# A decoder layer's two norms: token blocks multiplied before their norm, and norm weights applied per channel after the transposes

## Chip, cores and metric

The kernel runs on one core of a Trainium2 chip. The metric is device time in microseconds (us) for one execution. TensorE (PE) multiplies matrices and transposes, VectorE (DVE) and ScalarE (ACT) work elementwise, GpSimd (POOL) does small odd jobs, SyncE (SP) issues most of the transfers. SBUF is the on-chip memory, PSUM the eight banks that PE writes; a bank here holds 128 partitions x 512 float32.

## What is computed

One layer on 512 tokens of 1024 channels: an RMS norm, a combined input projection, a convolution branch and a gated linear attention branch, a gated merge with an output projection and a residual, a second RMS norm, a gated feed-forward of width 2816 with a short convolution, a residual, a last norm. The change touches the two norms and what reads them:

```python
def _rmsnorm(x, g):
    y = x * lax.rsqrt(jnp.mean(x * x, axis=-1, keepdims=True) + EPS)
    return y * g

u = _rmsnorm(h, norm1_g)
proj = u @ w_in                 # [conv GLU | q | k | v | r | decay | gates]
...
h = h + merged @ w_o
u2 = _rmsnorm(h, norm2_g)
z = _causal_dwconv(u2 @ w_ffn_up, ffn_dw_w, ffn_dw_b)
```

## The kernel before

Every float32 product is made of three fast ones: each operand is split into a high part (`hi`, a cast by ACT) and a remainder (`lo`, a subtraction by DVE), and `mm3` (L294) multiplies lo*hi, hi*lo and hi*hi into one bank. The tokens are four blocks of 128. Weights come as tiles of 128x1024 (512 KB): SP loads them into `raw` (four buffers), ACT casts `whi` (L253), DVE subtracts `wlo` (L256), and the load that takes the freed buffer is issued behind that. `order` fixes the sequence of weights, `split_weight` and `prefetch` keep the splits ahead of the products.

The start is ordered by hand for PE, ACT, DVE and SP (`manual_schedule`, L393). SP loads the first norm's weights as one row, x of block 0, two tiles of w_v, x of block 1, further weights. PE spreads the row over 128 partitions with two matmuls (L404) and does three warm-up matmuls (L408). `norm1(t)` squares and sums x (ACT, L413), adds epsilon (DVE), raises to -0.5 (POOL, L346) and multiplies x by the root and the weights (DVE, L419). `to_channels` (L369) transposes a block (PE, L375, two banks of four 128x128 pieces), casts (ACT, L379) and subtracts (DVE, L380) into `u1`, which holds hi and lo of all tokens by channel. `values(0, next_tokens)` then makes the first 512 columns of v: block by block, each over all eight channel groups with the four w_v tiles, 96 products; behind the fourth channel group of each block the next one is transposed and the one after it normed. Then come the GLU weights with all 512 tokens as the moving operand.

The output projection runs through `seven` (L823), a scheme of seven products on quarters: steps a11, a12, s1, n2, s4, n3, a22. Each step takes two token blocks (i = 0, 1); s4, n3 and a22 end with twelve products for each block, in banks x, y and z. A finished bank is added to or taken from `hres`, the residual stream (DVE, L870), and n3 and a22 write the banks x one after the other. `hres` is loaded again from x by SP (L881), behind the second norm's weights, which SP loads spread over 128 partitions (`load_gain`, 512 KB). `o_complete` squares and sums (ACT, L886) and takes the root (POOL); `norm2` multiplies by root and weights (DVE, L898); `o_at` places block 0's and 1's scaling behind n3's first block and their transposes behind a22's two blocks. The last w_o pieces are summed in memory by POOL's accumulating transfers (`kept`, L224).

The feed-forward's first group multiplies four tiles of w_up (L1044 to L1051) by the first 256 tokens and then by the last 256, since blocks 2 and 3 are normed last; these are transposed behind the third and fourth tile's first half.

## Time and profile before

| | before |
|---|---|
| median of 3 runs | 846.5 us (846.46 to 846.63) |
| profiled execution, span | 845.6 us |
| PE busy | 830.7 us (98%) |
| DVE busy | 646.0 us (76%) |
| ACT busy | 383.2 us (45%) |
| POOL busy | 42.6 us (5%) |
| first product of w_v starts at | 10.69 us |
| first product of w_glu starts at | 36.43 us |

The span reaches from the first to the last instruction of one profiled execution; the runs' times are taken without a profile. In a row by time stand start, duration, engine, line, operation, output <- input, shape, count, and in brackets the idle time before it and what ended that. In a row by group stand busy time, mean ns of one, and the idle time before. In a row by stretch stand the stretch, its length, busy time (and count) of PE, weight load, DVE, ACT and POOL, the granted clock of TensorE as a share of full speed, the transfers' share and GB/s. A matmul's duration is longer than the step to the next one, since they overlap. A float32 matmul that is not of the fast kind shows as two records.

### The profile page before, as it was taken

The page shows a single profiled execution, that of the slowest core. Times are in us where ns is not written, and L with a number is a line of the kernel's source. Part 1 is how long each engine was busy: PE and PEld are TensorE (multiplying, and loading weights), DVE is VectorE, ACT ScalarE, POOL GpSimd, SP SyncE. Part 2 cuts the span into 40 slices and gives each one's busy share as a digit, 9 for nine tenths or more (in the row PEclk, how much of TensorE's full clock was granted, in tenths as well). Part 3 has the DMA queues.
Part 4 walks back from the last instruction along what each step waited for, and adds up shares of the span by engine and source line. Part 5 has one row for each costly group of instructions (what it writes and reads, how often), then busy time and mean ns, then how long its engine had stood idle before and what let it go on. Part 6 is the DMA issues. An engine that isn't in the chain of part 4 may idle for free.

```text
span 845.6 us, 9983 instructions
## 1 busy us (share of the span) xinstructions
PE 830.7 (98%) x3826; PEld 691.0 (82%) x3826; DVE 646.0 (76%) x916; ACT 383.2 (45%) x533; POOL 42.6 (5%) x64
## 2 busy tenths in 40 slices
PE   8999999999999999999999899999999999999996
PEld 5888888888888888888888788888888888888885
DVE  5479879999998798744679648778767777677795
ACT  5433337535443522459335427444334443444454
POOL 1000000000100100000001100000100010000011
PEclk9999999999999999999999999999999999999999
DMA  8323222222222322222348533325832249222462
GB/s 293 110 93 102 90 104 87 93 94 83 93 75 75 124 100 100 87 88 75 125 106 213 179 125 120 106 76 112 224 126 100 66 90 274 101 93 99 100 124 101
DMA packets 28579, 97.79 MB, mean 116 GB/s; under 512 B 3233, under 2 KB 3617, under 8 KB 28530
## 3 DMA queue, kind: packets, MB, share of 16 engines
q1 hardware_dynamic: 25074, 85.35, 29.0%
q0 software_dynamic: 3456, 11.80, 8.0%
q8 instruction: 30, 0.49, 0.2%
q14 instruction: 19, 0.16, 0.1%
HBM read 95.03 MB, written 2.10 MB: 115 GB/s over the span
## 4 chain that ended last, share of the span: by engine, by line
PE 87%; DMA 4%; issue 3%; DVE 2%; ACT 1%; POOL 1%; SPq 0%; POOLq 0%; ACTq 0%; DVEq 0%
PE mm L299 27%; PE mm L298 27%; PE mm L300 27%; DMA kept<-in_w_o_dram 2%; DMA raw<-in_w_down_dram 1%; DMA hres<-in_x_dram 1%; PE ax L705 1%; DMA raw<-in_w_v_dram 1%; PE ax L707 1%; PE ax L687 1%; DVE hres L870 1%; DVE wlo L238 0%; PE ax L674 0%; PE ax L722 0%; ACT junk L990 0%
## 5 line engine op out<-in xcount | busy, mean ns | idle before, releaser
L298 PE MATMUL mm<-uh,wlo 128*128 128x512 f32 (+1 forms) x768 | 294.4, 384 | 1.2 <-DVE wlo L256 0.6
L299 PE MATMUL mm<-ul,whi 128*128 128x512 f32 (+1 forms) x768 | 292.1, 381 | 0.2 <-DVE ul L380 0.2
L300 PE MATMUL mm<-uh,whi 128*128 128x512 f32 (+1 forms) x768 | 292.2, 381 | 0.0
L253 ACT CAST whi<-raw 128x1024 fp32r<-128x1024 f32 x116 | 120.9, 1046 | 130.0 <-PE mm L300 96.6
L256 DVE TENSOR_TENSOR wlo<-raw,whi 128x1024 fp32r<-128x1024 f32 x116 | 141.0, 1218 | 37.7 <-ACT whi L253 37.2
L298 PEld LDWEIGHTS mm<-uh,wlo 128*128 128x128 f32 x768 | 144.2, 188 | 28.7 <-ACT uh L379 1.0
L299 PEld LDWEIGHTS mm<-ul,whi 128*128 128x128 f32 x768 | 144.5, 188 | 27.7 <-DVE ul L380 0.6
L300 PEld LDWEIGHTS mm<-uh,whi 128*128 128x128 f32 x768 | 144.4, 188 | 27.8
L464 DVE SCALAR_TENSOR_TENSOR c<-h,pp,c 128x511 f32<-128x511 f32 (+14 forms) x240 | 162.4, 729 | 0.7
L936 DVE SCALAR_TENSOR_TENSOR tmp<-mm,pp,tmp 128x511 f32<-128x511 f32 x88 | 65.8, 748 | 66.0 <-ACT tmp L934 64.8
L934 ACT ACTIVATE tmp<-mm,pp 128x512 f32<-128x512 f32 x44 | 34.3, 779 | 63.0 <-PE mm L300 63.0
L237 ACT CAST whi<-kept 128x1024 fp32r<-128x1024 f32 (+1 forms) x32 | 31.7, 994 | 26.4 <-PE mm L300 10.4
L238 DVE TENSOR_TENSOR wlo<-kept,whi 128x1024 fp32r<-128x1024 f32 (+1 forms) x32 | 36.7, 1152 | 3.1 <-ACT whi L237 2.8
L870 DVE TENSOR_TENSOR hres<-hres,mm 128x512 f32<-128x512 f32 (+1 forms) x49 | 32.7, 671 | 4.9 <-PE mm L300 3.7
L237 ACT CAST whi<-raw 128x1024 fp32r<-128x1024 f32 (+1 forms) x24 | 23.7, 995 | 19.4 <-PE mm L300 18.0
L238 DVE TENSOR_TENSOR wlo<-raw,whi 128x1024 fp32r<-128x1024 f32 (+1 forms) x24 | 27.3, 1152 | 3.2 <-ACT whi L237 3.2
L298 PE MATMUL mm<-whi,ul 128*128 128x512 f32 x64 | 25.3, 395 | 1.3 <-DVE ul L380 1.3
L346 POOL TENSOR_TENSOR rstd<-var,mhalf 128x1 f32<-128x1 f32 (+1 forms) x16 | 14.2, 891 | 243.4 <-DVE var L712 196.5
L299 PE MATMUL mm<-wlo,sh 128*128 128x512 f32 x66 | 25.8, 391 | 0.0
L300 PE MATMUL mm<-whi,sh 128*128 128x512 f32 x66 | 25.7, 389 | 0.0
L298 PE MATMUL mm<-whi,sl 128*128 128x512 f32 x66 | 25.5, 389 | 0.0
L298 PE MATMUL mm<-h,wlo 128*128 128x512 f32 x64 | 25.4, 397 | 0.0
(228 smaller groups left out, 1129.8 us busy)
## 6 DMA issues: line engine op xcount, KB each, us to landing
raw<-in_w_up_dram SPq DMA_DIRECT2D x44, 512.0 KB, 3.3
raw<-in_w_glu_dram SPq DMA_DIRECT2D x16, 512.0 KB, 3.4
raw<-in_w_down_dram SPq DMA_DIRECT2D x15, 512.0 KB, 3.2
kept<-in_w_down_dram POOLq DMA_DIRECT2D x10, 512.0 KB, 5.3
raw<-in_w_v_dram SPq DMA_DIRECT2D x8, 512.0 KB, 3.8
raw<-in_w_qk_dram SPq DMA_DIRECT2D x8, 512.0 KB, 3.3
raw<-in_w_r_dram SPq DMA_DIRECT2D x8, 512.0 KB, 3.2
raw<-in_w_gb_dram SPq DMA_DIRECT2D x8, 512.0 KB, 3.3
```

Of the source, the lines that this page charges most:

```text
L237: nc.scalar.copy(hi, raw)
L238: nc.vector.tensor_tensor(lo, raw, hi.bitcast(F32), ALU.subtract)
L253: nc.scalar.copy(hi, raw)
L256: pace[0] = nc.vector.tensor_tensor(lo, raw, hi.bitcast(F32), ALU.subtract)
L298: nc.tensor.matmul(acc, ll, rh, start=first, stop=False, **kw)
L299: nc.tensor.matmul(acc, lh, rl, start=False, stop=False, **kw)
L300: nc.tensor.matmul(acc, lh, rh, start=False, stop=last, **kw)
L346: nc.gpsimd.tensor_tensor(r, v, mhalf[:, :n], ALU.pow)
L464: nc.vector.scalar_tensor_tensor(y[:, s:], c[:, : T - s], w, y[:, s:], ALU.mult, ALU.add)
L870: nc.vector.tensor_tensor(hres[t, n][:, c], hres[t, n][:, c], bank[of[step]][i][:, c], op)
L934: nc.scalar.activation(z, acc, AF.Identity, bias=pp[:, PP_FB + m : PP_FB + m + 1], scale=w[2])
L936: nc.vector.scalar_tensor_tensor(z[:, s:], acc[:, : T - s], w[j], z[:, s:], ALU.mult, ALU.add)
```

## The change

Start. Both norms' weights are loaded as rows of 128 by ACT's queue and transposed once into `gains`, one column per channel group. SP's order becomes x0, w, x1, w, w, x2, w, x3; blocks 2 and 3 have room from the beginning. Ten warm-up matmuls of `ones` stand in place of three of the identity. Blocks 0 and 1 are transposed as they are (`turned`), weighted per channel from the bank (`gained`), split (`split_plain`) and multiplied without their root; the finished values get it from ACT (`v_done` with r). Later `renormed` spreads the root over the partitions with a small matmul, multiplies the kept weighted block by it and splits it into `u1` for the other products. Blocks 2 and 3 are scaled by their root (`shrunk`, DVE), transposed, and weighted in eight pieces of 128x128 each (`spread_gain`: ACT writes hi with the weight as scale, DVE writes lo). Products go by weight tile rather than by block (`v_block`), at times with the two that need `wlo` last.

Second norm. No spread weights are loaded. ACT scales by the root (`scaled`), `to_channels` weights in eight pieces, and the transposes move: block 0's behind n3, block 1's behind a22's first block, blocks 2 and 3's behind the second and third tile.

```diff
...
@@ -35,9 +35,9 @@
 AHEAD = 4
 LOOK = 2
 RATE = 5.0
-WARM = 3
+WARM = 10
 MID = 4
-PADS = (448, 2016, 768)
+PADS = (384, 2016, 768)
...
@@ -366,86 +367,212 @@
...
-    def to_channels(un, u, t, groups=(0, 1)):
-
+    def turned(x, spare=None):
+        banks = [ax_bank(), spare or ax_bank()]
+        for g in range(2):
+            for k in range(4):
+                nc.tensor.transpose(banks[g][:, k * P : (k + 1) * P], x[g][:, k * P : (k + 1) * P], ident)
+        return banks
+
+    def spread_gain(banks, which, dst, groups=(0, 1)):
         for g in groups:
-            tr = ax_bank()
-            for k in range(4):
-                c = (g * 4 + k) * P
-                nc.tensor.transpose(tr[:, k * P : (k + 1) * P], un[:, c : c + P], ident)
-            tr3 = tr.rearrange("p (k t) -> p k t", k=4)
-            uh = u[g][0][:, :, t * P : (t + 1) * P]
-            ul = u[g][1][:, :, t * P : (t + 1) * P]
-            nc.scalar.copy(uh, tr3)
-            nc.vector.tensor_tensor(ul, tr3, uh.bitcast(F32), ALU.subtract)
+            c = which * KT + g * 4
+            parts = [
+                (*dst(g, k), banks[g][:, k * P : (k + 1) * P], gains[:, c + k : c + k + 1]) for k in range(4)
+            ]
+            for hi, _, tr, gain in parts:
+                nc.scalar.activation(hi, tr, AF.Copy, scale=gain)
+            for hi, lo, tr, gain in parts:
+                nc.vector.scalar_tensor_tensor(lo, tr, gain, hi.bitcast(F32), ALU.mult, ALU.subtract)
+
+    def to_channels(x, u, t, which):
+        part = lambda g, k: tuple(u[g][i][:, k, t * P : (t + 1) * P] for i in range(2))
+        spread_gain(turned(x), which, part)
+
+    def scaled(x, r, dst=None):
+        dst = dst or x
+        for g in range(2):
+            nc.scalar.activation(dst[g], x[g], AF.Copy, scale=r)
+        return dst
+
...
 
 
     u1 = new_acts()
-    row = tp.tile([P, D], F32, tag="gain", name=nm("row"), bufs=1)[0:1, :]
     nc.vector.memset(ones, 1.0)
     nc.gpsimd.memset(mhalf, -0.5)
     xs = {}
 
     def load_x(t):
-        xs[t] = tp.tile([P, D], F32, tag="x", name=nm("x"), bufs=3)
-        nc.sync.dma_start(xs[t], a["x"][t * P : (t + 1) * P, :])
+        if t < 3:
+            x = tp.tile([P, D], F32, tag="x", name=nm("x"), bufs=3)
+            xs[t] = two(x)
+            nc.sync.dma_start(x, a["x"][t * P : (t + 1) * P, :])
+        else:
+            xs[t] = [heap(), heap()]
+            for j in range(2):
+                nc.sync.dma_start(xs[t][j], a["x"][t * P : (t + 1) * P, j * T : (j + 1) * T])
 
     start = tc.manual_schedule(engines=START)
     start.__enter__()
-    nc.sync.dma_start(row, a["norm1_g"].unsqueeze(0))
+    rows8 = tp.tile([P, D], F32, tag="gain", name=nm("row"), bufs=1)
+    for i, name in enumerate(("norm1_g", "norm2_g")):
+        nc.scalar.dma_start(rows8[i * KT : (i + 1) * KT, :P], a[name].rearrange("(k p) -> k p", p=P))
+    nc.scalar.activation(junk(P), ones, AF.Square)
     load_x(0)
-    load()
     load()
     load_x(1)
     load()
-
-    gain1 = [mm_bank(), mm_bank()]
-    for j in range(2):
-        nc.tensor.matmul(gain1[j], ones[0:1, :], row[:, j * T : (j + 1) * T], start=True, stop=True)
+    load()
+    load_x(2)
+    load()
+    load_x(3)
 
     warm = ax_bank()
     for _ in range(WARM):
-        nc.tensor.matmul(warm[:, :P], ident, ident, start=True, stop=True)
-
-    def norm1(t):
-        xt = xs[t]
-        ss = small(1, "ss")
-        nc.scalar.activation(junk(D), xt, AF.Square, scale=1.0 / 32.0, accum_out=ss)
+        nc.tensor.matmul(warm[:, :P], ones, ones, start=True, stop=True)
+    turned_gain = ax_bank()
+    nc.tensor.transpose(turned_gain[:, : 2 * KT], rows8[: 2 * KT, :P], ident[: 2 * KT, : 2 * KT])
+    nc.vector.tensor_copy(gains, turned_gain[:, : 2 * KT])
+
+    def rms(t):
+        ss = small(2, "ss")
+        for j in range(2):
+            nc.scalar.activation(junk(T), xs[t][j], AF.Square, scale=1.0 / 32.0, accum_out=ss[:, j : j + 1])
         v = small(1, "var")
-        nc.vector.tensor_scalar(v, ss, EPS, None, ALU.add)
-        r = rsqrt(v, 1)
-        for j in range(2):
-            s = slice(j * T, (j + 1) * T)
-            nc.vector.scalar_tensor_tensor(xt[:, s], xt[:, s], r, gain1[j], ALU.mult, ALU.mult)
-
-    norm1(0)
-    split_weight()
-    split_weight(lambda: to_channels(xs[0], u1, 0, (0,)))
-    to_channels(xs[0], u1, 0, (1,))
-    load_x(2)
-    norm1(1)
-    split_weight()
-    split_weight()
-    load_x(3)
+        nc.vector.scalar_tensor_tensor(v, ss[:, 0:1], EPS, ss[:, 1:2], ALU.add, ALU.add)
+        return rsqrt(v, 1)
+
+    plain, r1 = {}, {}
+
+    banks = {}
+
+    def shrunk(t):
+        for x in xs[t]:
+            nc.vector.tensor_scalar(x, x, r1[t], None, ALU.mult)
+
+    unscaled = {}
+
+    def split_by(f, hi, lo):
+        nc.scalar.copy(hi, f)
+        nc.vector.tensor_tensor(lo, f, hi.bitcast(F32), ALU.subtract)
+
+    def by_token(x):
+        return x.rearrange("p (k t) -> p k t", t=P)
+
+    def gained(t, g):
+        f = unscaled[t, g] = heap()
+        gain = gains[:, g * 4 : g * 4 + 4].unsqueeze(2).to_broadcast([P, 4, P])
+        nc.vector.tensor_tensor(by_token(f), by_token(banks[t][g]), gain, ALU.mult)
+
+    def split_plain(t, g):
+        plain[t, g] = (heap(F32R), heap(F32R))
+        split_by(unscaled[t, g], *plain[t, g])
+
+    def renormed(t):
+        rb = ax_bank()[:, :P]
+        nc.tensor.matmul(rb, r1[t].to_broadcast([P, P]), ident, start=True, stop=True)
+        rb = rb.unsqueeze(1).to_broadcast([P, 4, P])
+        for g in range(2):
+            f = unscaled[t, g]
+            nc.vector.tensor_tensor(by_token(f), by_token(f), rb, ALU.mult)
+        for g in range(2):
+            f = unscaled[t, g]
+            split_by(by_token(f), *(u1[g][i][:, :, t * P : (t + 1) * P] for i in range(2)))
+
     acts1 = by_k(u1)
 
-    def next_tokens(t):
-        if t + 1 < NT:
-            to_channels(xs[t + 1], u1, t + 1)
-        if t + 2 < NT:
-            norm1(t + 2)
-
+    def tokens(t):
+        def normed(k):
+            return tuple(x[:, t * P : (t + 1) * P] for x in acts1[k])
+
+        return normed
+
+    def as_landed(t):
+        return lambda k: tuple(x[:, k % 4 * P : (k % 4 + 1) * P] for x in plain[t, k // 4])
+
+    accs = [mm_bank() for _ in range(NT)]
+    ws = []
+
+    def v_block(j, *ts, low_last=False):
+        for t in ts:
+            src = as_landed(t) if t < 2 else tokens(t)
+            last = []
+            for i in range(2):
+                k = 2 * j + i
+                c = slice(i * T, (i + 1) * T)
+                w = (ws[j][0][:, c], ws[j][1][:, c])
+                if low_last:
+                    ah, al = src(k)
+                    nc.tensor.matmul(accs[t], al, w[0], start=k == 0, stop=False)
+                    nc.tensor.matmul(accs[t], ah, w[0], start=False, stop=False)
+                    last.append((ah, w[1]))
+                else:
+                    mm3(accs[t], src(k), w, k == 0, k == KT - 1)
+            for ah, wl in last:
+                nc.tensor.matmul(accs[t], ah, wl, start=False, stop=False)
+
+    def block_ready():
+        ws.append(weight("w_v", len(ws), 0))
 
     vt = {}
 
-    def v_done(t, n, acc):
+    def v_done(t, n, acc, r=None):
         vt[t, n] = heap()
-        nc.scalar.copy(vt[t, n], acc)
+        if r is None:
+            nc.scalar.copy(vt[t, n], acc)
+        else:
+            nc.scalar.activation(vt[t, n], acc, AF.Copy, scale=r)
+
+    here = lambda t: (lambda g, k: tuple(u1[g][i][:, k, t * P : (t + 1) * P] for i in range(2)))
+    banks[0] = turned(xs[0])
+    banks[1] = turned(xs[1], mm_bank())
+    gained(0, 0)
+    split_plain(0, 0)
+    gained(1, 0)
+    block_ready()
+    v_block(0, 0, low_last=True)
+    split_plain(1, 0)
+    v_block(0, 1)
+    block_ready()
+    gained(0, 1)
+    gained(1, 1)
+    split_plain(0, 1)
+    v_block(1, 0, 1, low_last=True)
+    split_plain(1, 1)
+    block_ready()
+    v_block(2, 0, 1, low_last=True)
+    r1[2] = rms(2)
+    shrunk(2)
+    banks[2] = turned(xs[2])
+    block_ready()
+    r1[3] = rms(3)
+    shrunk(3)
+    r1[0] = rms(0)
+    spread_gain(banks[2], 0, here(2))
+    v_block(3, 0, 1)
+    banks[3] = turned(xs[3])
+    v_block(0, 2)
+    v_block(1, 2)
+    r1[1] = rms(1)
+    spread_gain(banks[3], 0, here(3))
+    renormed(0)
+    v_done(0, 0, accs[0], r1[0])
+    v_done(1, 0, accs[1], r1[1])
+    v_block(0, 3)
+    v_block(1, 3)
+    renormed(1)
+    prefetch(1)
+    v_block(2, 2, 3)
+    prefetch(2)
+    v_block(3, 2, 3)
+    for t in range(2, NT):
+        v_done(t, 0, accs[t])
 
     def values(n, middle):
         row_half("w_v", n * KT // 2, n, acts1, KT, v_done, n == 1, middle)
 
-    values(0, next_tokens)
     start.__exit__(None, None, None)
     tp.tile([P, PADS[2] // 4], F32, name=nm("pad"))
     load_consts()
@@ -872,7 +999,6 @@
                             complete(t, n, c)
 
 
-    gain2 = load_gain("norm2_g")
     hres = {}
     ss2 = {}
     for t in range(NT):
@@ -892,32 +1018,24 @@
         return rsqrt(v, 1)
 
     def norm2(t, r):
-        un = tp.tile([P, D], F32, tag="x", name=nm("un"), bufs=3)
-        for j in range(2):
-            s = slice(j * T, (j + 1) * T)
-            nc.vector.scalar_tensor_tensor(un[:, s], hres[t, j], r, gain2[:, s], ALU.mult, ALU.mult)
-        return un
-
-    normed, roots = {}, {}
+        un = two(tp.tile([P, D], F32, tag="x", name=nm("un"), bufs=3))
+        return scaled([hres[t, 0], hres[t, 1]], r, un)
+
+    normed = {}
 
     def o_complete(t, n, c):
         square_sum(("n2", t), hres[t, n], n)
         if n == (0 if t > 1 else 1):
-            roots[t] = total_rstd(("n2", t))
-            if t > 1:
-                normed[t] = norm2(t, roots[t])
+            normed[t] = norm2(t, total_rstd(("n2", t)))
 
     u2 = []
 
     def o_at(step, i):
-        if (step, i) == ("n3", 0):
-            for t in range(2):
-                normed[t] = norm2(t, roots[t])
+        if (step, i) == ("n3", 1):
+            u2.extend(new_acts())
+            to_channels(normed[0], u2, 0, 1)
         if (step, i) == ("a22", 0):
-            u2.extend(new_acts())
-            to_channels(normed[0], u2, 0)
-        if (step, i) == ("a22", 1):
-            to_channels(normed[1], u2, 1)
+            to_channels(normed[1], u2, 1, 1)
 
     seven("w_o", O_PAIRS, mixed, o_complete, o_at)
     acts2 = by_k(u2)
@@ -1046,8 +1164,8 @@
             for lo in (0, T // 2):
                 for j, (w, acc) in enumerate(zip(ws, accs)):
                     col_tile(w, acts2, acc, lo, lo + T // 2)
-                    if lo == 0 and j > 1:
-                        to_channels(normed[j], u2, j)
+                    if lo == 0 and 1 <= j <= 2:
+                        to_channels(normed[j + 1], u2, j + 1, 1)
             early = {pairs[0][0]: accs[:2], pairs[0][1]: accs[2:]}
 
         def both(i):
```

More of the change, by code (lines that the diff above doesn't have):

```diff
@@ L121, in trunk_layer @@
     make_identity(nc, ident)
+    gains = cp.tile([P, 2 * KT], F32, name="gains")
     pp = cp.tile([P, PP_N], F32, name="pp")
@@ L367, in by_k, with two @@
         return [(u[k // 4][0][:, k % 4, :], u[k // 4][1][:, k % 4, :]) for k in range(KT)]
-    def to_channels(un, u, t, groups=(0, 1)):
-        for g in groups:
-            tr = ax_bank()
-            for k in range(4):
-                c = (g * 4 + k) * P
-                nc.tensor.transpose(tr[:, k * P : (k + 1) * P], un[:, c : c + P], ident)
-            tr3 = tr.rearrange("p (k t) -> p k t", k=4)
-            uh = u[g][0][:, :, t * P : (t + 1) * P]
-            ul = u[g][1][:, :, t * P : (t + 1) * P]
-            nc.scalar.copy(uh, tr3)
-            nc.vector.tensor_tensor(ul, tr3, uh.bitcast(F32), ALU.subtract)
+    def turned(x, spare=None):
[5 more added lines that the diff above has]
+    def spread_gain(banks, which, dst, groups=(0, 1)):
+        for g in groups:
+            c = which * KT + g * 4
[14 more added lines that the diff above has]
+        return dst
+    def two(x):
+        return [x[:, :T], x[:, T:]]
     u1 = new_acts()
-    row = tp.tile([P, D], F32, tag="gain", name=nm("row"), bufs=1)[0:1, :]
     nc.vector.memset(ones, 1.0)
```

## The prediction

> **What bounds the kernel now.** I read the totals first, then what TensorE waited for, then the order of time at the two places that the change touches, and last the durations by shape.
>
> ```profile
> span 845.6 us, 9983 instructions
> PE 830.7 (98%) x3826; PEld 691.0 (82%) x3826; DVE 646.0 (76%) x916; ACT 383.2 (45%) x533; POOL 42.6 (5%) x64
> ```
>
> ```profile
> PE mm L298 <- DVE hres L870: 2.8, 2, 2.3
> PE mm L404 <- DMA row<-in_norm_g_dram: 2.4, 1, 2.4
> PE mm L298 <- DVE ul L380: 1.3, 1, 1.3
> ```
>
> TensorE (PE) is busy 98% of the span, so the program is a queue of matmuls, and only their number and the holes between them count. The change leaves the number of products alone. The waits (us in total, times, longest) name the holes: one before the first product, and one of 2.3 us at L870, behind the second norm. Nothing in between can be gained.
>
> The first hole, in order of time (start, duration, engine and line):
>
> ```profile
> 0.81 0.36 SPq L395 DMA_DIRECT2D row<-in_norm_g_dram  x1
> 1.22 0.36 SPq L391 DMA_DIRECT2D x<-in_x_dram  x1
> ...
> 4.44 1.06 ACT L413 ACTIVATE junk<-x 128x1024 bf16<-128x1024 f32 x1 [2.36 <-DMA x<-in_x_dram]
> ...
> 6.09 1.65 PE L408 MATMUL ax<-ident 128*128 128x128 f32 x6
> ...
> 7.53 1.91 PE L375 MATMUL ax<-ident,x 128*128 128x128 f32 x8
> ...
> 8.38 1.04 ACT L253 CAST whi<-raw 128x1024 fp32r<-128x1024 f32 x1 [1.55 <-DMA raw<-in_w_v_dram]
> ...
> 10.69 0.50 PE L298 MATMUL mm<-whi,ul 128*128 128x512 f32 x1 [1.25 <-DVE ul L380]
> ...
> 11.03 0.40 PE L299 MATMUL mm<-wlo,uh 128*128 128x512 f32 x1
> ...
> 21.05 1.04 PE L375 MATMUL ax<-ident,x 128*128 128x128 f32 x8
> ...
> 35.75 0.39 PE L298 MATMUL mm<-whi,ul 128*128 128x512 f32 x1
> 36.43 0.39 PE L298 MATMUL mm<-uh,wlo 128*128 128x512 f32 x1
> ```
>
> Block 0 of x lands at 4.42, yet its first product starts at 10.69: square sum, power, norm, transposes and split stand between. The 96 products of w_v's first half end where the first of w_glu starts, at 36.43. The last two rows are three matmuls apart: 0.68 / 3 = 0.227 us each. Eight transposes take 1.04.
>
> The second hole:
>
> ```profile
> 473.49 1.05 ACT L237 CAST whi<-kept 128x1024 fp32r<-128x1024 f32 x1 [2.47 <-DMA kept<-in_w_o_dram]
> ...
> 475.50 1.40 POOL L346 TENSOR_TENSOR rstd<-var,mhalf 128x1 f32<-128x1 f32 x1 [4.50 <-DVE var L891]
> ...
> 476.55 0.27 PE L375 MATMUL ax<-ident,un 128*128 128x128 f32 x1
> ...
> 476.94 1.41 DVE L898 SCALAR_TENSOR_TENSOR un<-hres,rstd,gain 128x512 f32<-128x512 f32 x2 [0.45 <-POOL rstd L346]
> 478.27 0.68 DVE L870 TENSOR_TENSOR hres<-hres,mm 128x512 f32<-128x512 f32 x1
> 479.10 0.47 PE L298 MATMUL mm<-whi,h 128*128 128x512 f32 x1 [2.29 <-DVE hres L870]
> ...
> 481.16 0.63 PE L299 MATMUL mm<-wlo,h 128*128 128x512 f32 x1
> ```
>
> ```profile
> 480.50:481.00 0.50, 0.50 (x3) 0.40 (x2) 0.44 (x2) 0.43 (x2) 0.00 (x0) 0.50 0.00 0
> ...
> 483.50:484.00 0.50, 0.50 (x5) 0.50 (x5) 0.47 (x1) 0.00 (x0) 0.00 (x0) 0.74 0.88 344
> ```
>
> VectorE (DVE) sits at L898 until GpSimd's power arrives at 476.9, scales block 1, and only then does L870, which empties the bank that step a22 wants. PE idles 2.29 us. Afterwards the granted clock (in the two rows by stretch, the figure after POOL) is 0.50 from about 480.4 to 483.7, 3.3 us, which costs 1.7 more. The feed-forward's first matmuls follow as their pieces come:
>
> ```profile
> 501.91 0.28 PE L298 MATMUL mm<-uh,wlo 128*128 128x256 f32 x1
> 502.15 0.28 PE L300 MATMUL mm<-uh,whi 128*128 128x256 f32 x1
> 502.27 1.04 PE L375 MATMUL ax<-ident,un 128*128 128x128 f32 x8
> 503.54 0.74 PE L298 MATMUL mm<-uh,wlo 128*128 128x256 f32 x4 [0.24 <-ACT uh L379]
> ```
>
> A matmul of 256 columns costs 0.12. At 503.54 the second column halves start; from there PE runs dense until the tail.
>
> **The change, part by part.** Durations by shape (mean ns after the busy us):
>
> ```profile
> L379 ACT CAST uh<-ax 128x512 fp32r<-128x512 f32 x16 | 8.9, 586 | 21.1 <-PE ax L375 20.9
> L716 ACT ACTIVATE o<-ax,rstd 128x256 f32<-128x256 f32 x16 | 6.5, 471 | 5.9 <-POOL rstd L346 5.9
> L1018 ACT ACTIVATE hres<-hres,rstd 128x512 f32<-128x512 f32 x2 | 1.4, 722 | 1.3 <-POOL rstd L1006 1.3
> ...
> L256 DVE TENSOR_TENSOR wlo<-raw,whi 128x1024 fp32r<-128x1024 f32 x116 | 141.0, 1218 | 37.7 <-ACT whi L253 37.2
> L380 DVE TENSOR_TENSOR ul<-ax,uh 128x512 fp32r<-128x512 f32 x16 | 10.5, 685 | 14.2 <-ACT uh L379 14.2
> L694 DVE SCALAR_TENSOR_TENSOR state<-state,dec,ax 128x256 f32<-128x256 f32 x8 | 3.8, 474 | 0.0
> L1014 DVE TENSOR_SCALAR y<-y,rstd 128x640 f32<-128x640 f32 x2 | 1.1, 554 | 1.7 <-POOL rstd L1006 1.7
> L248 DVE TENSOR_TENSOR whi<-raw,whi 128x128 fp32r<-128x128 f32 x1 | 0.3, 283 | 0.0
> ```
>
> *The new price* is a 128x128 piece with its scale per channel: eight of ScalarE (ACT) and eight of DVE for a block where two of 128x512 stood. The trace has no such activation. From above it is bounded by L716 (0.47 for 256 columns), from below by taking 128 columns off that at L1018's slope ((0.72 - 0.47) / 2 = 0.125): 0.35 as a duration, some 0.26 from start to start when instructions overlap. For DVE, L248's 0.28 and L694's 0.47. I take 0.30 on both, near the lower end, since L248 has the very shape.
>
> *The start.* The gain row's DMA leaves SP's queue (both norms' weights come as 16 short rows over ACT's queue, behind nothing), so x0 goes out at 0.81 instead of 1.22 and lands at 4.0. x1 moves from fourth to third; the third transfer landed at 8.36 before, so x1 lands at 7.95. Ten warm matmuls (20 records at up to 0.25, from 1.65 us for six) fill PE until about 6, and x0's eight transposes end by 7.1; neither matters, because x1's eight stand in PE's order ahead of the first product. That makes 7.95 + 1.04 + a step = 9.05 for the first product; ACT has cast w0 by 8.6, in time. Then PE has 96 x 0.227 = 21.8, sixteen transposes 2.1, two broadcasts of the root 0.4: 24.3 together. The holes: DVE does x1's weighting (queued ahead of wlo) 8.7 to 9.4 and wlo 9.4 to 10.6, while the four products that need no wlo last until 9.96, so 0.7; x1's split behind it 0.15; wlo of w2 0.3, behind four weightings and splits; wlo of w3, behind the scaling of x2 (0.45 a half by L1014), 0.4. Sum 9.05 + 24.3 + 1.55 = 34.9, against 36.43: **-1.5**. ACT's square sums, the 32 small pieces of x2 and x3, and the later rescaling of blocks 0 and 1 lie beside products: chained by the same durations, DVE ends block 1's split at 32.2 and w_glu's first wlo at 33.7 to 34.2, before 34.9. That slack of about 1 us is what this cover is worth. At 0.26 a piece the start is 34.7; at 0.47 it is 37.3.
>
> *The second norm.* Its gain's 512 KB load goes (no wait of PE hangs on it), and the scaling moves from DVE to ACT, so DVE's wait for the power goes to ACT's queue. Block 0 is scaled by 472.5, before ACT's cast of the last w_o piece at 473.49. DVE splits that 474.6 to 475.8 and reaches L870's work at 476.5. PE: eight transposes of block 0 from 476.55 to 477.6, then a22's first twelve to 480.3. **The 2.29 us hole is gone.** What is late next: ACT, which holds the wait for the power (until 477.3), then two scalings (0.65 each) to 478.7, a square sum 0.76, w_up's cast 0.97 to 480.4, four pieces to 481.6; DVE its wlo to 481.7 and four pieces to 482.9. Block 1's second four transposes need the bank that these free, so PE stands from 480.8 to 483.0: a new hole of 2.1 us. Then 0.5 + 2.7 (a22's second half) to 486.3, by which time block 1 is split; 96 x 0.12 + sixteen transposes 2.1 + 0.3 for block 2's scaling = 13.9: the second halves start at 500.2. Block 3's split, before behind the last first-half tile, now hides under it, so they run without the 0.24. 500.2 against 503.54 + 0.24: **-3.5**. At 0.26 and a power of 0.55 it is 498.9, at 0.47 it is 502.8. ACT's heavier load does not reach PE later: from there orders match.
>
> **Sum:** 845.6 - 1.5 - 3.5 = 840.6; the runs' median stands 0.9 above the profiled execution, which makes **841.5**.
>
> **A rule of the skill.** Between the last warm matmul (6.09 + 1.65 = 7.7) and 10.69 the trace has only transposes and idle, 3.0 us, and from 11.03 the products run at full rate (0.40). In the Trainium skill, "TensorE: Matmul & The Clock Gate", section "Part 4: PE-mode transpose", it is stated that transposes do not count as busy for the gate. The new start has a like stretch, from 6 to 9.05. If the gate closed there, one window of 3.3 us at 0.50 would fall on the first products, 1.7 more: 843.2. The trace lost nothing behind such a stretch, so I go by the row and give this 0.04.
>
> **The rivals.**
> 1. *The new hole costs a window of clock.* The hole of 2.29 us was followed by 3.3 us at 0.50; mine of 2.1 is nearly as long. For it: the rows of 480.5. Against: it may fall across two windows, and other holes (1.25 at 10.69) cost nothing. 1.7 back: 843.2. The Trainium skill, "TensorE: Matmul & The Clock Gate", "HAM oscillation", asks for idle gaps over 3.4 us before the gate closes; by it this rival could not be. The 2.29 us hole disagrees.
> 2. *The blocks are not multiplied as they land*: the first product waits for x1, and x1 lands where it did (9.66 less 0.41 = 9.25, by the rows below). Everything in the start moves by 1.3: 842.8, with the start worth 0.2.
>
> ```profile
> 2.56 0.43 SPq L391 DMA_DIRECT2D x<-in_x_dram  x1
> ...
> x<-in_x_dram SPq DMA_DIRECT2D x1, 512.0 KB, 7.1
> ```
>
> 3. *The hole at a22 stays*, because the last w_o piece lands 2 us later (ACT's cast waited 2.47 for it already): only the start is gained, 845.0.
> 4. *Slower: ACT becomes the bound.* If a small piece costs 0.47, L716's whole price, the start loses 0.9 and the second norm gains 0.9: even. That is the point. At 0.53, the step of two 128x512 copies, the start is 38.3 (+1.9) and the second halves start at 504.1 (+0.3): 848.7.
>
> **How the numbers follow.** Forecast 0.50, rival 1 0.18, the gate at the start 0.04, rival 2 0.12, rival 3 0.08, rival 4 0.08. Faster by over 0.2% (1.7 us, about what can be told from no change) means below 844.8: the forecast, both clock cases and rival 2, 0.84; rival 3 is the same, rival 4 slower. Low end: 0.26 a piece and quick powers, -1.7 and -4.9, 839.9; the high end takes in rival 3, 845.2. The forecast's own range is 839.8 to 843.0.
>
> **What would show it.** In the changed profile: first product near 9.05; first of w_glu near 34.9; small pieces near 0.35 each, 0.30 apart; no wait of PE on the residual's addition, but one of about 2 us on DVE or a bank at block 1's transposes; second halves starting some 5 us earlier than 503.5; the granted clock in the 10 us behind 479. Wrong if x1 lands after 8.6, if pieces stand over 0.45 apart, or if anything but these two stages changes length.

## The result, and the profile after

| | before | after |
|---|---|---|
| median of 8 runs each | 846.1 us (845.3 to 848.5) | 841.6 us (840.8 to 844.7) |
| ratio after / before | | 0.9951 (95% interval 0.9938 to 0.9963) |
| profiled execution, span | 845.6 us | 839.8 us |

The changed kernel is faster by 0.5%. The page of after, its totals:

```profile
span 839.8 us, 10108 instructions
PE 829.0 (99%) x3841; PEld 692.3 (82%) x3841; DVE 650.0 (77%) x953; ACT 397.6 (47%) x590; POOL 45.0 (5%) x64
```

Behind the start, one of TensorE's waits (us in total, times, longest) is new:

```profile
PE ax L849 <- ACT o L843: 1.1, 1, 1.1
```

The wait on the residual's addition behind the second norm is gone. The new one is a wait of the attention heads, at 200 us. In order of time, the start (start, duration, engine and line):

```profile
5.90 1.71 PE L374 MATMUL ax<-ident,x 128*128 128x128 f32 x8
...
8.12 0.63 PE L374 MATMUL ax<-ident,x 128*128 128x128 f32 x4 [0.52 <-DMA x<-in_x_dram]
...
9.40 0.51 PE L508 MATMUL mm<-whi,h 128*128 128x512 f32 x1 [0.21 <-ACT whi L254]
...
20.51 2.15 ACT L384 ACTIVATE uh<-ax,gains 128x128 fp32r<-128x128 f32 x8
...
34.80 0.39 PE L299 MATMUL mm<-uh,wlo 128*128 128x512 f32 x1
```

First product 1.29 us earlier than before, first product of w_glu 1.63 earlier. Then the heads:

```profile
194.41 4.80 POOL L347 TENSOR_TENSOR rstd<-var,mhalf 128x2 f32<-128x2 f32 x2 [114.05 <-DVE var L839]
...
199.24 0.84 ACT L843 ACTIVATE o<-ax,rstd 128x256 f32<-128x256 f32 x2 [2.90 <-POOL rstd L347]
...
199.77 1.13 PE L849 MATMUL ax<-ident,o 128*128 128x128 f32 x6 [1.06 <-ACT o L843]
...
206.23 0.60 PE L794 MATMUL ax<-ident,k 128*128 128x128 f32 x4
```

The same place before:

```profile
195.98 1.84 POOL L346 TENSOR_TENSOR rstd<-var,mhalf 128x2 f32<-128x2 f32 x2 [113.99 <-DVE var L712]
...
199.96 1.04 PE L722 MATMUL ax<-ident,o 128*128 128x128 f32 x8
...
206.33 0.60 PE L667 MATMUL ax<-ident,k 128*128 128x128 f32 x4
```

Two powers of GpSimd that took 1.84 us together took 4.80, ScalarE's scaling came late, TensorE stood. At 206 us the lead was 0.10: the start's whole gain was lost in this execution, in a place that the diff does not touch. The second norm:

```profile
473.31 1.23 DVE L239 TENSOR_TENSOR wlo<-kept,whi 128x1024 fp32r<-128x1024 f32 x1 [0.46 <-ACT whi L238]
...
474.45 0.15 DVE L1017 SCALAR_TENSOR_TENSOR var<-ss 128x1 f32<-128x1 f32 x1
...
474.52 0.68 DVE L997 TENSOR_TENSOR hres<-hres,mm 128x512 f32<-128x512 f32 x1
...
474.75 0.55 POOL L347 TENSOR_TENSOR rstd<-var,mhalf 128x1 f32<-128x1 f32 x1 [3.79 <-DVE var L1017]
...
475.34 1.34 ACT L395 ACTIVATE un<-hres,rstd 128x512 f32<-128x512 f32 x2 [1.44 <-POOL rstd L347]
...
476.27 0.39 PE L301 MATMUL mm<-whi,sums 128*128 128x512 f32 x1
...
476.51 1.03 PE L374 MATMUL ax<-ident,un 128*128 128x128 f32 x8
...
477.30 0.48 PE L299 MATMUL mm<-whi,h 128*128 128x512 f32 x1
...
480.12 1.18 PE L374 MATMUL ax<-ident,un 128*128 128x128 f32 x8
...
509.33 0.40 PE L299 MATMUL mm<-uh,wlo 128*128 128x512 f32 x1
```

TensorE goes from n3's last product (476.27) through block 0's transposes, a22 and block 1's transposes without a stop. The last row, the first 512-column product behind the feed-forward's first group, stood at 515.41 before. The granted clock was 1.00 in every stretch from 470 to 506; before, it was at half behind the hole.

The profiled pair thus differs by -1.63 (up to 34.80), +1.59 (from there to n3's end), -6.04 (to the first 512-column product) and +0.28 (to the end): -5.80.

### The profile page after: what moved, and what is told of

Same layout as the page of the kernel before. It is cut to its first block, busy times and chain, and to the rows that moved or that the text cites. A ratio compares the mean times of both kernels' runs of the same rounds, so it can differ in the third digit from the quotient of the medians.

```text
span 839.8 us, 10108 instructions
## 1 busy us (share of the span) xinstructions
PE 829.0 (99%) x3841; PEld 692.3 (82%) x3841; DVE 650.0 (77%) x953; ACT 397.6 (47%) x590; POOL 45.0 (5%) x64
## 4 chain that ended last, share of the span: by engine, by line
PE 87%; DVE 9%; ACT 1%; issue 1%; POOL 1%; POOLq 0%; ACTq 0%; DVEq 0%
PE mm L299 26%; PE mm L301 26%; PE mm L300 26%; DVE c L591 4%; DVE wlo L257 2%; PE ax L301 1%; PE ax L300 1%; PE ax L299 1%; POOL rstd L347 1%; PE ax L832 1%; PE ax L374 1%; PE ax L434 1%; PE ax L814 0%; PE ax L834 0%; PE ax L849 0%
## 5 line engine op out<-in xcount | busy, mean ns | idle before, releaser
L347 POOL TENSOR_TENSOR rstd<-var,mhalf 128x1 f32<-128x1 f32 (+1 forms) x16 | 16.6, 1046 | 239.3 <-DVE var L839 194.8
L225 POOL DMA_DIRECT2D kept<-in_w_down_dram x12 | 10.4, 863 | 272.9 <-DVE wlo L239 272.9
```

What stands on the lines that cost most here:

```text
L347: nc.gpsimd.tensor_tensor(r, v, mhalf[:, :n], ALU.pow)
```

## Experiments

All but one compute the whole layer. Times are medians; the kernel before was timed beside each call (844.9, 846.5 and 845.6).

Where the table below gives stages, G is the start of the first w_glu product, N the step behind n3's last product (its start plus 0.24), F the start of the first 512-column product behind the first group; all read from rows like those above. "Powers" is what the two powers near 195 us took together.

| kernel, one profile each | G | G to N | N to F | F to end | powers |
|---|---|---|---|---|---|
| before | 36.43 | 440.12 | 38.86 | 330.19 | 1.84 |
| before_again | 36.86 | 440.13 | 36.16 | 330.25 | 1.84 |
| start_only | 34.44 | 440.18 | 36.17 | 330.81 | 1.78 |
| norm_only | 36.98 | 441.74 | 33.20 | 330.38 | 4.87 |
| after | 34.80 | 441.71 | 32.82 | 330.47 | 4.80 |
| again | 34.46 | 440.18 | 32.91 | 331.65 | 1.78 |
| gain_load | 34.45 | 446.17 | 32.82 | 330.16 | 6.67 |
| scale_dve | 34.62 | 440.95 | 32.59 | 330.84 | 1.78 |
| late_turn | 33.85 | 440.73 | 35.27 | 330.45 | 1.78 |
| x0_first | 38.44 | 441.59 | 32.82 | 330.75 | 4.80 |
| psum_gap | 34.60 | 440.18 | 32.82 | 330.50 | 2.17 |
| again2 | 34.15 | 440.18 | 32.81 | 330.46 | 1.78 |
| gap_scale | 34.63 | 440.22 | 32.59 | 330.46 | 2.18 |

**before_again and again**: both kernels unchanged, to see what in the first two profiles was theirs and what was one execution's.

> The kernel before, unchanged, against itself. One theory: the 2.3 us hole of TensorE at the residual addition behind the second norm, and the 3.3 us at clock 0.50 behind it, come every time; then the span is again near 845.6 and the second halves of the feed-forward's first group start near 503.5. Rival: the hole is fixed by the code and comes again, but the half clock comes in some executions only; then a profile without it has a span near 843.9 (845.6 less 1.7), and the gain of the change by spans of 845.6 and 839.8 is 1.7 too large. The ratio should be 1.000, within 0.001.

> The changed kernel, unchanged. In its first profile the lead of 1.6 us from the start was lost near 198 us, where two powers of GpSimd took 4.8 us together (1.84 in the kernel before) and TensorE waited 1.06 us for the scaling behind them. Theory: this is a chance event of one execution; the powers take about 2 us here, there is no wait, the lead holds up to the second norm, and the span is near 838.3. Rival: it comes from the earlier start every time (another instruction of VectorE runs when the power does); the powers take over 4 us again, and the span is 839.8. Time 841.5 by the rival, nearer 840 by the theory.

before_again: 845.6, ratio 1.0003 (0.9993 to 1.0013). Its profile has the hole, but half as long, and no half clock:

```profile
472.68 1.05 ACT L237 CAST whi<-kept 128x1024 fp32r<-128x1024 f32 x1 [1.21 <-DMA kept<-in_w_o_dram]
...
474.54 0.15 DVE L891 SCALAR_TENSOR_TENSOR var<-ss 128x1 f32<-128x1 f32 x1
474.61 1.22 DVE L238 TENSOR_TENSOR wlo<-kept,whi 128x1024 fp32r<-128x1024 f32 x1
...
474.83 1.41 POOL L346 TENSOR_TENSOR rstd<-var,mhalf 128x1 f32<-128x1 f32 x1 [3.40 <-DVE var L891]
...
476.28 1.42 DVE L898 SCALAR_TENSOR_TENSOR un<-hres,rstd,gain 128x512 f32<-128x512 f32 x2 [0.45 <-POOL rstd L346]
477.61 0.68 DVE L870 TENSOR_TENSOR hres<-hres,mm 128x512 f32<-128x512 f32 x1
...
478.44 0.47 PE L298 MATMUL mm<-whi,h 128*128 128x512 f32 x1 [1.18 <-DVE hres L870]
```

The reader sees the chain that makes the hole: variance, a subtraction of VectorE, the power that lasts until just behind it (1.41), the scaling, the addition. So 2.7 us of the 38.86 (half clock and 1.1 of hole) belonged to the one execution. What was longer there is in the rows too: ScalarE waited 2.47 for the transfer of the last w_o piece and cast it 3.1 us before n3's last product ended; here it waited 1.21 and cast it 4.3 before, and the variance of block 1 came that much sooner. The rest of the hole is VectorE's: in start_only below, the cast stands 4.8 before and the hole is 1.17 all the same.

again: 840.1, 0.9939 (0.9922 to 0.9956); the powers took 1.78, no wait, and G to N is 440.18. The long powers were an event of the execution, as the theory said. The span, 839.2, was not the 838.3 expected: F to end is 1.2 longer here, which the table shows of no other profile of this kernel. Most of that hangs on another such piece, now of the down projection, for which ScalarE waited 2.52 (1.23 in again2):

```profile
699.93 0.62 ACT L238 CAST whi<-kept 128x512 fp32r<-128x512 f32 x1 [2.52 <-DMA kept<-in_w_down_dram]
...
702.02 0.47 PE L299 MATMUL mm<-whi,al 128*128 128x512 f32 x1 [0.94 <-DVE hres L997]
```

No other profile of this kernel has a hole of TensorE over 0.15 there.

**start_only and norm_only**: the changed kernel with the old second norm (`load_gain`, scaling by VectorE, wide transposes in their old places), and the kernel before with the new second norm:

```diff
+    for i, name in enumerate(("norm1_g", "norm2_g")):
+        nc.sync.dma_start(rows8[i * KT : (i + 1) * KT, :P], ...)
+    nc.tensor.transpose(turned_gain[:, : 2 * KT], rows8[: 2 * KT, :P], ...)
+    nc.vector.tensor_copy(gains, turned_gain[:, : 2 * KT])
```

> The new start with the old second norm (spread weights loaded, scaling by VectorE, transposes where they were). If the lead of the start (1.6 us at w_glu's first product) reaches the end: 844.5 against 846.1. If the powers near 198 us eat it every time: 846.0, with a lead of about 0.1 us behind 206 us in the trace. First w_glu product at 34.8 either way; hole of 2.3 us at the residual addition as before.

> The old start with the new second norm (both weights loaded and turned behind the start). By the spans of the two first profiles the second norm gains 5.6 us: 840.5 against 846.1. If the half clock behind the hole is not there in most executions of the kernel before, 3.9 us: 842.2. By the prediction's own sum 3.5: 842.6. No wait of TensorE at block 1's transposes, a power near 0.55 us and the last w_o piece cast without a wait, if the first profile's reading holds.

start_only 843.0, 0.9976 (0.9963 to 0.9990), 1.9 us less than before: the lead reaches the end. The hole of the old second norm was 1.17 in its profile, not the 2.3 expected. norm_only 842.9, 0.9972 (0.9959 to 0.9985), 2.1 less, which is under all three of its forecasts (3.5 to 5.6). Its profile has the long powers with the old start (which the diff of the start therefore does not cause). N to F is 36.17 with the old second norm and 33.20 with the new: about 3 us, close to the prediction's 3.5 and not the 6.0 of the first pair.

**gain_load, scale_dve, late_turn**: what in the second norm does it.

```diff
+    load_gain("norm2_g")          # gain_load
     hres = {}
...
-        return scaled([hres[t, 0], hres[t, 1]], r, un)
+        for g in range(2):        # scale_dve
+            nc.vector.tensor_scalar(un[g], hres[t, g], r, None, ALU.mult)
+        return un
...
-        if (step, i) == ("n3", 1):
+        if (step, i) == ("a22", 0):        # late_turn
             to_channels(normed[0], u2, 0, 1)
-        if (step, i) == ("a22", 0):
+        if (step, i) == ("a22", 1):
             to_channels(normed[1], u2, 1, 1)
...
-                    if lo == 0 and 1 <= j <= 2:
-                        to_channels(normed[j + 1], u2, j + 1, 1)
+                    if lo == 0 and j > 1:
+                        to_channels(normed[j], u2, j, 1)
```

> The changed kernel with the 512 KB of spread weights of the second norm loaded again, in their old place ahead of the residual stream; nothing reads them. Theory: this load shares the transfer engines (full from 460 to 472) with the last w_o piece and delays it, so the cast of that piece waits again for its transfer (by 1 us or more; no wait without the load), the scaling of block 1 comes about a microsecond later than 1.2 us before n3's last product, and a hole of up to 1 us opens at block 1's transposes; from n3's last product to the first 512-column product behind the first group 33.3 to 34 us, against 32.8 and 32.9 in the two profiles of the changed kernel and 36.2 in undisturbed ones of the kernel before. Rival: the load hangs on nothing; 32.9.

> The changed kernel with the second norm's scaling by VectorE (two 128x512 tensor-scalar, about 0.44 each as in the start) instead of ScalarE; transposes and small pieces stay. By the prediction's step, VectorE waiting for the power was what made the 2.3 us hole at the residual addition, so a wait of 1 us or more comes back at that addition: 34 or more from n3's last product to the first 512-column product. Rival: the hole came from the late last w_o piece and from a power that ran under a subtraction of VectorE (1.40 against 0.55 us); with the piece early and the power quick VectorE is free before n3's last product ends, and there is no hole: 32.9, with ScalarE relieved of 1.3 us.

> The changed kernel with the transposes in their old places (block 0 and 1 behind a22's two blocks, blocks 2 and 3 behind the third and fourth tile). Theory: the early transposes hide the eight small pieces of a block (2.2 us on ScalarE, as much on VectorE a little later); without them TensorE waits about 2 us before the first w_up product and about 2 us before the second halves, where the kernel before lost 1.2 and 0.24 in all: 36 to 37 from n3's last product to the first 512-column product. Rival: removing VectorE's wait for the power is all there is to it, and the places matter little: 33.5.

gain_load (840.3, 0.9925, 0.9904 to 0.9947): N to F 32.82, the last w_o piece cast without a wait. The theory about the load falls; in this profile it costs nothing. scale_dve (841.3, 0.9935, 0.9913 to 0.9957): the rival is right, there is no hole, N to F 32.59:

```profile
473.78 0.15 DVE L1017 SCALAR_TENSOR_TENSOR var<-ss 128x1 f32<-128x1 f32 x1
473.85 0.68 DVE L997 TENSOR_TENSOR hres<-hres,mm 128x512 f32<-128x512 f32 x1
...
474.08 0.56 POOL L347 TENSOR_TENSOR rstd<-var,mhalf 128x1 f32<-128x1 f32 x1 [4.00 <-DVE var L1017]
...
474.67 0.88 DVE L1023 TENSOR_SCALAR un<-hres,rstd 128x512 f32<-128x512 f32 x2
...
476.35 0.48 PE L299 MATMUL mm<-whi,h 128*128 128x512 f32 x1
```

VectorE still scales, but behind the addition, and the power beside an addition that reads PSUM takes 0.56, not 1.41. So it is the order on VectorE, not the engine that scales: in the profiles of the old second norm block 1's scaling stands ahead of n3's first addition, in those of the new one behind it. The text of the kernel does not show this order (the new `o_complete` asks for the scaling ahead of that addition, as the old `o_at` did); the traces do. No run changes the order alone.

late_turn (844.1, 0.9966, 0.9946 to 0.9987): N to F 35.27, 2.4 more than with the early transposes. TensorE waits 0.85 ahead of four transposes, for ScalarE's scaling, just before the first w_up product, then 0.21, 0.31 and 0.42 for splits; no hole comes back at the addition. Neither end of the expectation held (36 to 37, or 33.5). By this run 2.4 of the second norm's 3.3 us hang on the places of the transposes. The other 0.9 are what all the rest of the change there makes together, the closed hole and the dearer small pieces among it; no run divides them.

**x0_first**: whether block 1's transposes ahead of the first product cost anything.

```diff
     banks[0] = turned(xs[0])
-    banks[1] = turned(xs[1], mm_bank())
     gained(0, 0)
     split_plain(0, 0)
-    gained(1, 0)
     block_ready()
     v_block(0, 0, low_last=True)
+    banks[1] = turned(xs[1], mm_bank())
+    gained(1, 0)
     split_plain(1, 0)
```

> The changed kernel with block 0's first six products placed ahead of block 1's transposes. By the prediction's step the first product waits for x1 and its transposes (9.05 forecast); then it comes here about 1 us earlier and w_glu's first product up to 0.5 us earlier. Rival: the first product waits for ScalarE's cast of the first w_v tile, which is as late as the transposes are (0.21 of wait in the first profile); then it moves by less than 0.3, block 1's weighting and split come later, and w_glu's first product is the same or up to 0.8 later.

845.0, 0.9973 (0.9953 to 0.9993): the start is 4 us worse (G 38.44), where the rival had allowed 0.8. By time, and the granted clock by stretch:

```profile
9.33 0.50 PE L508 MATMUL mm<-whi,h 128*128 128x512 f32 x1 [1.94 <-ACT whi L254]
...
14.82 0.50 PE L299 MATMUL mm<-whi,h 128*128 128x512 f32 x1 [1.31 <-DVE h L459]
```

```profile
10.00:11.00 1.00, 1.00 (x4) 0.51 (x3) 0.54 (x1) 0.00 (x0) 0.00 (x0) 0.59 1.04 426
11.00:12.00 1.00, 1.00 (x4) 0.70 (x4) 0.00 (x0) 0.00 (x0) 0.00 (x0) 0.50 1.01 381
12.00:13.00 1.00, 1.00 (x7) 1.00 (x6) 0.30 (x1) 0.00 (x0) 0.00 (x0) 0.50 1.01 368
```

The first product does not come earlier, as the rival said: ScalarE's cast of the first w_v tile ends at 9.3 too. The transposes fill a hole that is there anyway, keep block 1 ready, and without them the hole (1.94) is followed by some 3 us at half clock, in which TensorE has few products that can run.

**pow_alone**: why a power takes 0.55, 1.4 or several us. The layer is left out; `op` is the stage's VectorE instruction.

```diff
+    for i, (op, many, powers) in enumerate(stages):
+        nc.vector.tensor_scalar(v, root, 2.0, None, ALU.add)
+        for n in range(powers):
+            root = roots[:, 2 * n : 2 * n + 2]
+            nc.gpsimd.tensor_tensor(root, v, mhalf, ALU.pow)
+        for _ in range(many):
+            op()
```

> The layer is left out: nine stages in which GpSimd raises 128x2 values to -0.5 six times (four in the first stage) while VectorE is idle, or runs one kind of instruction back to back: three-operand 128x512 in SBUF, tensor-tensor 128x512 and 128x1024 in SBUF, tensor-scalar 128x512 in SBUF, then the same kinds with one operand in PSUM, and the first again. Theory (GpSimd is held by a VectorE instruction with its operands in SBUF and gets in between two of them only by chance): about 0.5 each when VectorE is idle and when an operand lies in PSUM; 0.6 to over 2 and uneven, or not before the stage's VectorE work ends, with two operands in SBUF. Rival (the 4.8 and 6.7 us were something else, such as the transfers or the fetching of code): about the same 0.5 to 0.9 in every stage.

GpSimd by time, one row a stage (four or six powers each), the first seven of nine:

```profile
2.29 2.65 POOL L112 TENSOR_TENSOR roots<-v,mhalf 128x2 f32<-128x2 f32 x4 [1.46 <-DVE v L109]
5.23 5.06 POOL L112 TENSOR_TENSOR roots<-v,mhalf 128x2 f32<-128x2 f32 x6 [0.28 <-DVE v L109]
16.20 4.74 POOL L112 TENSOR_TENSOR roots<-v,mhalf 128x2 f32<-128x2 f32 x6 [5.91 <-DVE v L109]
26.37 7.95 POOL L112 TENSOR_TENSOR roots<-v,mhalf 128x2 f32<-128x2 f32 x6 [5.42 <-DVE v L109]
36.45 4.69 POOL L112 TENSOR_TENSOR roots<-v,mhalf 128x2 f32<-128x2 f32 x6 [2.13 <-DVE v L109]
48.96 3.94 POOL L112 TENSOR_TENSOR roots<-v,mhalf 128x2 f32<-128x2 f32 x6 [7.83 <-DVE v L109]
60.03 3.94 POOL L112 TENSOR_TENSOR roots<-v,mhalf 128x2 f32<-128x2 f32 x6 [7.13 <-DVE v L109]
```

VectorE idle: 0.66 a power (2.65 / 4). With one operand in PSUM (last two rows, and the eighth stage with 3.94 for six) the same, 0.66. With all operands in SBUF 0.78 to 0.85 beside 128x512 (the ninth stage, 5.12, among them) and 1.33 beside 128x1024: one power for each three-operand or tensor-tensor instruction, six powers in nine of the shorter tensor-scalars. So a power waits for VectorE's running instruction when that has its operands in SBUF. But here it gets in between any two; the long waits of 3 us and more over several instructions did not appear.

**psum_gap, again2, gap_scale**: whether that can be kept from happening.

```diff
                 r = rsqrt(v, 2)
+                gap = tp.tile([P, DV], BF16, tag="gap", name=nm("gap"), bufs=1)
+                nc.vector.tensor_scalar(gap, po[:, :DV], v[:, 0:1], None, ALU.mult)
```

> The changed kernel with one more VectorE instruction behind each variance of the attention heads: a 128x256 tensor-scalar that reads PSUM, whose result nobody uses. Theory: GpSimd's power gets in while VectorE reads PSUM (0.66 each beside such work, measured alone), so each pair of powers takes under 2 us in every execution, TensorE never waits 1 us or more for the heads' scaling, from w_glu's first product to n3's last product it is 440.2 each time, and the median lies about 0.5 to 1 us below the unchanged kernel's in this call, with a smaller spread. Rival: the long pairs come from something else; then they come as often (4 of 10 profiles so far), the median is the same or up to 0.5 us higher for VectorE's added 3 us.

> The changed kernel unchanged, beside the other two on the same chip. Median 840.1 to 841.6 by the calls before; in the profile either a long pair of powers near 194 us with a wait of TensorE (span near 839.8 to 843) or a short one (838 to 839).

> The added reads of PSUM and the second norm's scaling on VectorE together. If both hold: 440.2 from w_glu's first product to n3's last, 32.6 from there to the first 512-column product behind the first group (32.9 with ScalarE), and the median 0.3 us below the kernel with the reads alone. Rival: the scaling on VectorE, behind a power, takes back as much elsewhere: the same median.

839.9, 839.4 and 839.6, ratios 0.9934 (0.9922 to 0.9946), 0.9932 (0.9919 to 0.9944) and 0.9933 (0.9920 to 0.9947): the same. The pairs take 2.17 instead of 1.78, since the second variance waits behind the added read. No long pair came in any of the three, one of which has no such read, so whether the read prevents one stays open; the expected half to one microsecond did not show. gap_scale has the 32.59 and 440.22 that were expected, and no lower median. Neither beats the changed kernel that was timed beside it (again2).

## Why the prediction was right, and where it was not

The time, 841.6 against 841.5, and the sign came out. That it came so close is in part luck: the sum got there with two of its steps wrong in opposite directions, and the changed kernel's median was 840.1 and 839.4 in the two later calls.

- *Only holes in TensorE's queue count.* Right: PE's share went from 98 to 99%, and all differences are holes or half clock.
- *The start, -1.5.* Right in the first pair (-1.63), somewhat small over all: the mean of G is 36.76 in the three profiles of the old start and 34.44 in the nine of the new one as it stands, -2.3. 34.9 had been forecast for the new one, and 36.43 was the earliest of the old. x1's transposes began at 8.12 (7.95 forecast). The first product, forecast 9.05, came at 9.40 behind ScalarE's cast, and from 8.46 to 9.40 in the nine profiles. Eight small pieces take 2.15, with 0.38 for one by itself, so (2.15 - 0.38) / 7 = 0.25 apart: the lower bound held, not the 0.30 taken, and rival 4 (0.47) was out.
- *The second norm, -3.5.* Right among undisturbed executions (36.16 against 32.81 to 32.91, so -3.3), by the wrong way. The step that failed is "ACT, which holds the wait for the power (until 477.3)" and the 2.1 us hole drawn from it: the power ended at 475.3 and ScalarE's two scalings at 476.7. The cast of the last w_o piece came at 472.24 (not 473.49), VectorE now runs its subtraction ahead of the variance, and the power ran beside the addition where that subtraction in SBUF ran before; no hole opened. So the second halves start at 497.8 (509.33 - 96 x 0.12) instead of 500.2, 2.4 earlier than forecast, and the base had about as much too much: the 38.86 from which the prediction subtracted held 2.7 us of one execution's own.
- *The cause of the old hole.* The prediction had VectorE's wait for the power move to ScalarE's queue. scale_dve has the scaling on VectorE, behind the addition, and no hole: leaving VectorE was not needed.
- *The power at 1.40* was taken as a property of the place; it is a property of what VectorE runs beside it (1.40 or 1.41 in all three profiles of the old second norm, 0.55 or 0.56 in those of the new).
- *From there orders match; nothing else changes length.* Wrong in the profiled execution by +1.59 near 200 us. The order there is the same; GpSimd's powers came late, an event in 4 of 13 profiles of the layer, with either start. It costs about 1.5 us, and 6.0 in gain_load's profile, where the hole (2.94) brought half clock as well.
- *The 0.9 us between span and median.* In every run the time is 1.7 us above its own span (841.55 and 839.8; 845.12 and 843.4), so the profiled execution of before was one of about 847.3, 1.2 above that kernel's median. The 0.9 set this against the median and happened to fit.
- *Rivals.* The half clock (rival 1) was no danger here, as no hole opened. Rival 2 fell with x1's transposes at 8.12, rival 3 with the hole gone. The gate at the start (0.04): in the nine profiles of the new start as it stands no half clock follows the transposes; in x0_first it follows 1.94 us of nothing. But the row on which the 0.04 rested, full rate behind the old start's transposes, does not hold in every execution: in before_again, one of three profiles of that start, some ten products behind the same stretch ran at half rate (last section).

By stages and without such events the change is worth -2.3, 0, -3.3 and +0.2 (F to end): -5.4. The medians of the three calls that timed the changed kernel itself differ by 4.5, 4.8 and 6.2. Not tried: how the start's gain divides between the dropped row, the order of loads and the ten warm-up matmuls; and why scale_dve and late_turn lose 0.8 and 0.6 between G and N, where their profiles show waits of 0.44 and 0.21 for the split of a w_o piece near 453 us and the other profiles of the new kernel none.

## What to carry to other kernels

Where one engine is full, read a second profile of the unchanged kernel before you subtract from a stage: here one hole and the clock behind it were 2.7 us of a single execution. When a wait sits in front of an addition that frees a bank, first ask whether the addition can go ahead of it; changing the engine was not needed. A short GpSimd operation on the critical path wants VectorE reading PSUM, or idle, beside it.

## What the runs showed of the hardware

- *The granted clock and the length of a hole.* Holes of TensorE of 1.06 to 1.74 us in these profiles were followed by full clock; those of 1.94 (x0_first), 2.29 (before) and 2.94 (gain_load) by about 3 us or more at 0.50. gain_load around 200 us, by stretch:

```profile
200.00:202.00 2.00, 0.70 (x3) 0.52 (x4) 0.18 (x1) 1.23 (x4) 0.74 (x1) 0.66 0.69 242
202.00:204.00 2.00, 2.00 (x8) 1.79 (x7) 1.71 (x3) 1.98 (x3) 0.00 (x0) 0.50 0.07 25
204.00:206.00 2.00, 2.00 (x6) 1.54 (x5) 2.00 (x4) 1.99 (x5) 0.00 (x0) 0.50 0.00 0
```

  The Trainium skill, "TensorE: Matmul & The Clock Gate", "HAM oscillation", asks for idle gaps over about 3.4 us. These three disagree.
- *Half rate that the clock column does not show.* In before_again's start the products behind the one at 10.12 stand 0.43 apart until 14.55, twice the 0.227 of later ones:

```profile
10.71 0.63 PE L299 MATMUL mm<-wlo,uh 128*128 128x512 f32 x1
...
14.55 0.51 PE L299 MATMUL mm<-wlo,uh 128*128 128x512 f32 x1
```

  The column prints 1.00 for this stretch, but that is no reading: the trace has no clock record before 14.78, and 1.00 is printed where there is none. The first record, at full clock, stands at 9.31 in the first profile of before, at 9.58 in norm_only and at 4.42 to 7.20 in the ten profiles with ten warm-up matmuls. Ahead of it matmuls of 128 columns stand 0.21 apart in each of them, behind it 0.11. So all these executions begin at half rate, and the column is to be trusted from the first record on. With ten warm-up matmuls full rate came before the first product every time (products of 0.48 to 0.51 us); with three it came after it once in three. w_glu's first product came 0.43 later for it than in the first profile, though its first w_v product came 0.57 earlier.
- *GpSimd behind VectorE.* The Trainium skill, "SBUF — State Buffer", "Who interferes with whom", states that a VectorE instruction with two inputs in SBUF blocks a GpSimd instruction that reads SBUF for as long as it runs, and one with an input in PSUM does not. pow_alone agrees (1.33 and 0.66). What the runs add is that behind VectorE instructions without a gap between them a power can miss several turns. VectorE in the profile of after, while the second power lasts from 195.43 to 199.21:

```profile
194.89 2.69 DVE L591 SCALAR_TENSOR_TENSOR c<-h,pp,c 128x509 f32<-128x509 f32 x4
197.50 1.22 DVE L760 TENSOR_TENSOR_SCAN b<-run,h 128x512 f32<-128x512 bf16 x1
198.64 1.20 DVE L257 TENSOR_TENSOR wlo<-raw,whi 128x1024 fp32r<-128x1024 f32 x1
```

  In again VectorE ran the same instructions in the same order, and the second power ended 0.55 behind the one that was running when it began (0.76 in all); here it ended 0.49 behind the scan, the fifth. In gain_load, where the two took 6.67, it ended 0.56 behind the last instruction before VectorE fell idle. Why turns are missed in some executions and not in others was not found.
